# Remainders of projection weights: subtraction on two engines, or an accumulating DMA

## The chip, the cores and the metric

The kernel runs on one core of a Trainium2 chip. The metric is the device time of one execution in microseconds (us), the median of several runs. PE is TensorE (PEld its weight loads), DVE is VectorE, ACT is ScalarE, POOL is GpSimd, SP is SyncE, which here issues DMAs only.

## What is computed

A decoder of two layers for 512 tokens of 1024 columns. Layer 0 is a gated DeltaNet (projections to queries, keys, values and gates, a short convolution, a delta rule over chunks of 64 tokens), layer 1 a sparse attention with three branches over one shared set of keys and values. Each layer is modulated by a condition c. The core of the reference:

```python
for l in range(DEPTH):
    shift, scale, gate = ada_modulation(c, ada_w[l], ada_b[l])
    h = rmsnorm(x, norm_g[l]) * (1.0 + scale) + shift
    if l < N_A_LAYERS:
        out = gated_deltanet_layer(h, a_in_w[l], a_conv_w[l], a_A_log[l], a_dt_bias[l], a_onorm_g[l], a_out_w[l])
    else:
        j = l - N_A_LAYERS
        out = nsa_layer(h, shared, rel_bias, b_in_w[j], b_out_w[j])
    x = x + gate * out
    if l == N_A_LAYERS - 1:
        shared = nsa_shared_kv(x, kv_norm_g, kv_w, cmp_pos_k, cmp_pos_v, cmp_k_w1, cmp_k_w2, cmp_v_w1, cmp_v_w2)
return rmsnorm(x, final_g)
```

In both layers `h @ in_w` and `y @ out_w`, and `s @ kv_w` for the shared keys and values, are the large products: these are the projections that the change is about.

## The kernel before

**A projection's tile.** A projection is made in tiles of 128 columns. The weights of one are 1024 x 128 float32, 512 KB, and lie in SBUF as 128 partitions x 8 blocks x 128. A product of two float32 matrices is made from parts that PE multiplies in one pass: the weights are split into a rounded part `whi` (the type fp32r) and the remainder `wlo` = weights - `whi`, the other operand likewise into a high and a low part. `dense_steps` (L176) then makes 24 products of 128x512 a tile: for each of the 8 blocks whi with the high part (L186), wlo with the high part (L188) and whi with the low part (L190).

**Loading and splitting.** `load_w` (L155) issues the load of the raw weights `wraw` on SP's queue. `split_w` (L160) copies them to `whi` on ACT (L88 is the line of the helper `act`), and subtracts (L85 is the helper `tt`): a half of the blocks on DVE and the other half on POOL; with `on_pool=8`, as for values and queries of layer 0, all on POOL. wraw, whi and wlo have three buffers each; wraw's are shared with pieces `aw` of the modulation's weights.

**Who splits when.** Projections stand in a `chain` of `Ahead` objects (L235). Each is a generator that has two stages before its products: load, then split. When a projection emits its second product, it has the next one of the chain split; at its fourth, the one after the next loaded. `fill(n)` emits n products of the projections waiting in `todo`, among other work: convolutions, the inverse of the chunks' triangular matrices (L750 to L784), the scan, and in layer 1 the attention.

**What sets the order.** PE's order is that in which the code emits (a manual schedule). ACT's is, too, up to L782. The other engines' order is a scheduler's, which simulates the program. Each engine works its own list off in order; a DMA that POOL issues stands in POOL's list.

**The stages.** Up to some 60 us keys are projected; 62 to 105 us values; 105 to 215 us values, gates and queries beside the inverse (from 148 us on DVE does sums of products `arY`, `arX` of the inverse); then the scan; 335 to 407 us x1, the layer's output, of whose tiles the first three are split by a direct call of `split_w` and the other five pass through the chain; 407 to 465 us the shared keys and values; 465 to 790 us attention with 8 tiles of queries and 24 of gates; then the output projection x2.

**Who does not change.** The keys (split apart or by `dense`, with `ahead=False`), the branch gates (`gate_steps`), the first three tiles of x1 and the halves of x2's last tiles call the old way of splitting before and after.

Of the kernel before, what the change touches and what calls it, by code (L numbers as in the profile page):

```python
# [16 lines left out]
T = 512  # L17
# [40 lines left out]
def tile_hybrid_trunk(ctx: ExitStack, tc: tile.TileContext, A, out, dbg=None):  # L58
# [28 lines left out]
    def act(o, i, fn=AF.Copy, **kw):  # L87
        nc.scalar.activation(o, i, fn, **kw)  # L88
# [30 lines left out]
    class Shared:  # L119
        """Small tables of one phase, cut from a tile whose place the other phase takes over."""  # L120
# [39 lines left out]
    def split_w(raw, on_pool=4, parts=None, split=False):  # L160
        hi, lo = parts or (wp.tile([P, KT, P], F32R, name=n, bufs=3) for n in ("whi", "wlo"))
        q = 2 if split else KT
        act(hi[:, :q], raw[:, :q])
        if split:
            nc.vector.tensor_copy(hi[:, q:], raw[:, q:])
        h = KT - on_pool
        if split:
            tt(nc.vector, lo[:, :2], raw[:, :2], hi[:, :2].bitcast(F32), ALU.subtract)
            tt(nc.vector, lo[:, 2:h], raw[:, 2:h], hi[:, 2:h].bitcast(F32), ALU.subtract)
        elif h:  # L170
            tt(nc.vector, lo[:, :h], raw[:, :h], hi[:, :h].bitcast(F32), ALU.subtract)
        if h < KT:
            tt(nc.gpsimd, lo[:, h:], raw[:, h:], hi[:, h:].bitcast(F32), ALU.subtract)
        return hi, lo

    def dense_steps(src, xh, xl, name, on_pool=4, raw=None, parts=None, tag="d", done=None, ahead=True):  # L176
        """W^T x by single-pass products of the parts, one at a time."""
        raw = raw if raw is not None else load_w(src)
        if ahead:
            yield None  # L180
        wh, wl = split_w(raw, on_pool, parts)
        if ahead:
            yield None
        ps = (pd if tag == "d" else pm).tile([P, T], F32, name=name, tag=tag)
        for k in range(KT):
            nc.tensor.matmul(ps, wh[:, k], xh[:, k], start=(k == 0), stop=False)  # L186
            yield ps
            nc.tensor.matmul(ps, wl[:, k], xh[:, k], start=False, stop=False)  # L188
            yield ps
            nc.tensor.matmul(ps, wh[:, k], xl[:, k], start=False, stop=(k == KT - 1))  # L190
            if k == KT - 1 and done:
                done(ps)
            yield ps

    def gate_steps(src, xh, xl, name, done):
        """The branch gates' few columns, the parts of their weights side by side."""
        raw = load_w(src)
        yield None
        w = wp.tile([P, KT, P], F32R, name="whi", bufs=3)
        act(w[:, :, 0:64], raw[:, :, 0:64])  # L200
        tt(nc.vector, w[:, :, 64:128], raw[:, :, 0:64], w[:, :, 0:64].bitcast(F32), ALU.subtract)
        yield None
        ps = pd.tile([P, T], F32, name=name, tag="d")
        for k in range(KT):
            for x in (xh, xl):
                nc.tensor.matmul(ps, w[:, k], x[:, k], start=(k == 0 and x is xh), stop=(k == KT - 1 and x is xl))
                if k == KT - 1 and x is xl:
                    done(ps)
                yield ps
# [8 lines left out]
    def after(n, f):  # L218
        """Leaves f for when n more products of the waiting projections are out."""
        later.append((clock[0] + n, f))  # L220
# [14 lines left out]
    class Ahead:  # L235
        """A projection whose weights are split while the one before it runs."""
# [5 lines left out]
        def go(self, stage):  # L242
            """Up to loaded (1) or split (2) weights."""
            while self.stage < stage:
                next(self.steps)
                self.stage += 1
# [4 lines left out]
        def __next__(self):  # L251
            self.go(2)
            self.n += 1
            if self.n == 2 and self.i + 1 < len(chain):
                chain[self.i + 1].go(2)
            if self.n == 4 and self.i + 2 < len(chain):
                chain[self.i + 2].go(1)
            return next(self.steps)

    def fill(n):  # L260
        """Emits the next n products of the waiting projections."""
        while n > 0 and todo:
            if next(todo[0], None) is None:
                todo.pop(0)
            else:
                n -= 1
                tick()

    def residual(wsrc, h_, l_, gate, xin, xout, name, after, tags="dddddddd"):
        """xout = xin + gate * (W^T y) by column tiles; the sums of squares of all of them but the last, and the last's."""  # L270
        sums = []

        def done(j, ps):
            stt(xout(j), ps, gate[:, j:j + 1], xin(j), ALU.mult, ALU.add)
            sq = tmp(f"{name}sq{j}")
            act(sq, xout(j), AF.Square)
            if 0 < j < KT - 1:
                tt(nc.gpsimd, sums[0], sums[0], sq, ALU.add)
            else:
                sums.append(sq)  # L280
            after(j)

        return [dense_steps(wsrc[j], h_, l_, f"{name}{j}", tag=tags[j], done=partial(done, j)) for j in range(3, KT)], sums, done
# [3 lines left out]
    def rsqrt(dst, src, scale):  # L287
        """dst = (src * scale + eps) ** -0.5 on small tables: a first guess from the exponent, three Newton steps."""
# [23 lines left out]
    def chunk(src, cols, dst):  # L312
        """A block of a weight, all rows by some columns, two row tiles a transfer."""
# [6 lines left out]
    def vec_mat(vec, t, dst, bias, name, between=0):  # L320
        """dst = vec^T W + bias with columns onto partitions: four partial sums side by side, then their transposes."""
# [26 lines left out]
    def ada_piece(space=None):  # L348
        """The modulation's other columns, two row tiles of four column tiles at a time, off the tensor engine."""
# [122 lines left out]
    def shifted(i):  # L472
        """Half of the modulated input."""
# [6 lines left out]
    def again(i):  # L480
        """The keys' weights once more."""
# [56 lines left out]
    def ready(ct):  # L538
        """Waits for a convolved column tile."""
# [87 lines left out]
    def keys(i, part):  # L627
        """Half of the keys, with the shift."""
# [65 lines left out]
    def decay_prep(h, low):  # L694
        """The exponent's size (low) or itself (up) inside the triangle, out of range outside."""
# [55 lines left out]
    with tc.high_priority(offset=400):  # L751
          for b in (2, 4, 8, 16):
              n, st = 16 // b, 66 * b

              def prod(o, i0, i1, right):
                  """o[pair, c, a] = sum over m of i0[pair, a, m] * i1[pair, c, m]; (tile, offset, strides of pair, free, m).
                  The triangle is the right factor, no m under c, or the left one, no m over a."""
# [168 lines left out]
    def scan_norm(G, n0, n1):  # L926
        """The norm of the outputs of some chunks, with the queries' norm."""
# [8 lines left out]
    def scan_turn(n, G):  # L936
        """Heads onto partitions, gated."""
# [46 lines left out]
    with tc.high_priority(offset=300):  # L984
# [30 lines left out]
        def some(j, ks, c, stop):  # L1015
            """A part of a column tile's products."""
# [72 lines left out]
    def key_rows(t, dst):  # L1089
        """Both halves of the partitions get hi, in one copy, and lo, in the other."""  # L1090
# [87 lines left out]
    class Head:  # L1178
# [18 lines left out]
        def softmax(self, qb):  # L1197
            """Scores of a block of queries, with their bias, through the three softmaxes and the branch gates."""
# [39 lines left out]
        def turn(self, qb):  # L1238
            """Keys on partitions, four blocks a bank."""
# [64 lines left out]
    def to_rows(j, n0, n1):  # L1304
        """The last norm's gain, and tokens onto partitions."""
# [33 lines left out]
    def x2_steps(j, parts=None):  # L1339
        """A column tile of the output projection."""  # L1340
# [7 lines left out]
    def early():  # L1348
        """The output projection's first tiles over the pairs that are done."""
# [9 lines left out]
    def x2_halves():  # L1359
        """The last column tiles, half of the tokens after the other."""  # L1360
# [58 lines left out]
    with ordered:  # L1419
# [204 lines left out]
```

## Time and profile before

| | us |
|---|---|
| median of 3 runs (lowest to highest) | 833.56 (833.0 to 839.4) |
| span of the profiled execution | 834.3 |
| PE busy | 759.7 (91%) |
| DVE busy | 598.0 (72%) |
| ACT busy | 404.0 (48%) |
| POOL busy | 370.6 (44%) |
| chain that ended last: PE 65%, DVE 22%, DMA 5% | |

For the profiled execution the span is the only time on record. Busy times are of one execution; an engine that is idle costs nothing unless another waits for it, so the stages and the waits are read beside them. A row's L number is a line of the kernel before; in a row of a timeline the start counts from the span's beginning. A half remainder of 128x512 is a row `wlo<-wraw,whi 128x512`, a whole one `128x1024`.

### The profile page before, as it was taken

Reading aid. Unit: us, or ns where it says so; the run is one execution under the profiler, and the core shown is the slowest. Engines: PE = TensorE matmul, PEld = TensorE weight load, DVE = VectorE, ACT = ScalarE, POOL = GpSimd, SP = SyncE. Lnnn points to the kernel's source line nnn. Section 1 sums busy time; section 2 is a strip of 40 time slices with the busy share of each in tenths; the row PEclk is TensorE's granted clock in tenths of the full one; section 3 lists DMA queues with packets and bytes.
Section 4 is the critical chain, followed back from the end, with each engine's and each line's share of the span. In section 5 each row is a group of like instructions: output and inputs, shape, how many; then the busy total and the mean of one; then the engine's idle time right before and its main releaser. Section 6 shows DMA issues by size and latency. Waiting matters only on the chain.

```text
span 834.3 us, 13577 instructions
## 1 busy us (share of the span) xinstructions
PE 759.7 (91%) x4773; PEld 618.5 (74%) x4773; DVE 598.0 (72%) x1473; ACT 404.0 (48%) x921; POOL 370.6 (44%) x344
## 2 busy tenths in 40 slices
PE   4998779878899997999986999999999999999996
PEld 2675458657788886797774788888888888887876
DVE  2699596897246658879888487777776867768574
ACT  2543646553415553354434285547564745457222
POOL 2365134586733233315389243444444444446150
PEclk9999979899958999999998999999999999999999
DMA  8976133437632143147813432232322232323112
GB/s 305 386 218 213 50 104 79 147 132 199 160 116 76 51 166 113 53 138 223 334 51 112 131 98 90 89 90 71 95 89 63 92 99 80 103 73 115 51 38 101
DMA packets 52852, 104.20 MB, mean 125 GB/s; under 512 B 15930, under 2 KB 24474, under 8 KB 52784
## 3 DMA queue, kind: packets, MB, share of 16 engines
q1 hardware_dynamic: 43392, 97.19, 36.0%
q10 hardware_dynamic: 8720, 4.06, 1.8%
q0 software_dynamic: 672, 2.09, 0.9%
q8 instruction: 37, 0.61, 0.3%
q14 instruction: 31, 0.25, 0.1%
HBM read 97.49 MB, written 7.14 MB: 125 GB/s over the span
## 4 chain that ended last, share of the span: by engine, by line
PE 65%; DVE 22%; DMA 5%; issue 3%; ACT 2%; ACTq 1%; POOL 1%; SPq 0%; DVEq 0%
PE z L186 5%; PE z L190 5%; PE z L188 5%; PE o L1261 4%; PE pt L1245 4%; PE pc L186 3%; PE pc L188 3%; DVE wlo L85 2%; PE pc L190 2%; DVE arY L85 2%; DVE arK L82 2%; PE q L186 2%; PE q L188 2%; PE q L190 2%; DMA wraw<-in_wS 1%
## 5 line engine op out<-in xcount | busy, mean ns | idle before, releaser
L85 POOL TENSOR_TENSOR wlo<-wraw,whi 128x512 fp32r<-128x512 f32 (+2 forms) x84 | 140.3, 1672 | 180.3 <-ACT whi L88 136.9
L88 ACT ACTIVATE arX<-arX,nm 128x256 f32<-128x256 f32 (+3 forms) x128 | 71.2, 556 | 103.2 <-DVE nm L1202 102.5
L79 POOL TENSOR_SCALAR arX<-arX,f 128x256 f32<-128x256 f32 (+3 forms) x128 | 68.8, 550 | 97.8 <-DVE f L85 60.7
L88 ACT ACTIVATE whi<-wraw 128x1024 fp32r<-128x1024 f32 (+2 forms) x85 | 88.2, 1039 | 38.2 <-DMA wraw<-in_wA 11.5
L85 DVE TENSOR_TENSOR wlo<-wraw,whi 128x512 fp32r<-128x512 f32 (+2 forms) x69 | 72.6, 1055 | 11.3 <-ACT whi L88 11.1
L190 PE MATMUL z<-h1l,whi 128*128 128x512 f32 x192 | 76.8, 400 | 0.0
L186 PE MATMUL z<-h1h,whi 128*128 128x512 f32 x192 | 76.6, 399 | 0.0
L188 PE MATMUL z<-h1h,wlo 128*128 128x512 f32 x192 | 75.9, 395 | 0.0
L186 PE MATMUL pc<-xh,whi 128*128 128x512 f32 x128 | 57.3, 448 | 16.4 <-DVE vT L82 8.1
L190 PE MATMUL pc<-xl,whi 128*128 128x512 f32 x128 | 55.2, 431 | 1.1 <-DVE xl L85 1.1
L188 PE MATMUL pc<-xh,wlo 128*128 128x512 f32 x128 | 55.8, 436 | 0.1
L186 PEld LDWEIGHTS pc<-xh,whi 128*128 128x128 f32 x128 | 26.6, 208 | 27.3 <-issue 22.4
L1245 PE MATMUL pt<-ident,arX 128*128 128x128 f32 x320 | 45.3, 272 | 0.0
L1245 PEld LDWEIGHTS pt<-ident,arX 128*128 128x128 f32 x320 | 38.7, 140 | 8.3
L188 PEld LDWEIGHTS z<-h1h,wlo 128*128 128x128 f32 x192 | 36.2, 188 | 6.1
L186 PEld LDWEIGHTS z<-h1h,whi 128*128 128x128 f32 x192 | 36.2, 188 | 5.6
L190 PEld LDWEIGHTS z<-h1l,whi 128*128 128x128 f32 x192 | 36.1, 188 | 5.5
L85 POOL TENSOR_TENSOR ap<-ap,aw 128x512 f32<-128x512 f32 x21 | 31.2, 1485 | 9.9 <-ACT ap L88 7.7
L1202 DVE CUSTOM_DVE_ANT_0 arX<-sw,arY 128x256 f32<-128x256 f32 (+2 forms) x48 | 26.7, 557 | 11.0 <-POOL arX L79 6.6
L1261 PE MATMUL o<-pta,vb 128*64 128x128 f32 x336 | 32.1, 275 | 0.0
L1231 DVE TENSOR_SCALAR f<-sm 128x3 f32<-128x3 f32 x64 | 14.6, 228 | 24.3 <-ACT arX L88 24.1
L190 PEld LDWEIGHTS pc<-xl,whi 128*128 128x128 f32 x128 | 26.6, 208 | 6.7 <-DVE xl L85 1.5
(433 smaller groups left out, 2205.4 us busy)
## 6 DMA issues: line engine op xcount, KB each, us to landing
wraw<-in_wB SPq DMA_DIRECT2D x33, 512.0 KB, 3.3
wraw<-in_wA SPq DMA_DIRECT2D x28, 512.0 KB, 4.6
aw<-in_ada_w SPq DMA_DIRECT2D x20, 512.0 KB, 3.9
arY<-in_ada_w SPq DMA_DIRECT2D x12, 512.0 KB, 4.7
arN<-gcd SPq DMA_DIRECT2D x16, 256.0 KB, 3.8
wraw<-in_wO SPq DMA_DIRECT2D x8, 512.0 KB, 3.4
arY<-rbw SPq DMA_DIRECT2D x64, 64.0 KB, 2.0
wraw<-in_wP SPq DMA_DIRECT2D x8, 512.0 KB, 3.3
```

The costliest lines, as they stand in the source:

```text
L79: eng.tensor_scalar(out=o, in0=i, scalar1=s1, scalar2=s2, op0=op0, op1=op1)
L82: nc.vector.scalar_tensor_tensor(out=o, in0=i, scalar=s, in1=j, op0=op0, op1=op1)
L85: eng.tensor_tensor(out=o, in0=a, in1=b, op=op)
L88: nc.scalar.activation(o, i, fn, **kw)
L186: nc.tensor.matmul(ps, wh[:, k], xh[:, k], start=(k == 0), stop=False)
L188: nc.tensor.matmul(ps, wl[:, k], xh[:, k], start=False, stop=False)
L190: nc.tensor.matmul(ps, wh[:, k], xl[:, k], start=False, stop=(k == KT - 1))
L1202: nc.vector.tensor_tensor_reduce(out=o, in0=ps, in1=bias, op0=ALU.add, op1=ALU.min, scale=1.0, scalar=init, accum_out=acc)
L1231: nc.vector.tensor_scalar_max(f[:, qb], sm[:, qb], 1e-30)
L1245: nc.tensor.transpose(self.ps[:, i], x[:, kb * P:(kb + 1) * P], ident)
L1261: nc.tensor.matmul(po[64 * e:64 * e + 64, qb * P:(qb + 1) * P], vv, pts[2 * pr + e, br, kb, qb], start=(kb == 0), stop=(kb == qb), tile_po ...
```

## The change

`split_w` gets the address of the weights in memory. Where it has it, ACT makes `whi` as before and then a second copy, -whi, into `wlo`; then POOL issues a DMA that reads the weights from memory once more and adds them to `wlo`. The subtractions on DVE and POOL are gone there. `dense_steps` passes the address if the projection is in the chain. And `Ahead` splits the next projection at the first product, the one after it at the second, and loads the third at the fourth. The rest of the diff takes comments out and moves lines by up to 7.

```diff
-    def split_w(raw, on_pool=4, parts=None, split=False):
+    def split_w(raw, on_pool=4, parts=None, split=False, src=None):
         hi, lo = parts or (wp.tile([P, KT, P], F32R, name=n, bufs=3) for n in ("whi", "wlo"))
+        if src is not None:
+            act(hi, raw)
+            act(lo, hi.bitcast(F32), scale=-1.0)
+            nc.gpsimd.dma_start(lo, src, accum_op=ALU.add)
+            return hi, lo
         q = 2 if split else KT
...
-        wh, wl = split_w(raw, on_pool, parts)
+        wh, wl = split_w(raw, on_pool, parts, src=src if ahead else None)
...
             self.go(2)
             self.n += 1
-            if self.n == 2 and self.i + 1 < len(chain):
+            if self.n == 1 and self.i + 1 < len(chain):
                 chain[self.i + 1].go(2)
-            if self.n == 4 and self.i + 2 < len(chain):
-                chain[self.i + 2].go(1)
+            if self.n == 2 and self.i + 2 < len(chain):
+                chain[self.i + 2].go(2)
+            if self.n == 4 and self.i + 3 < len(chain):
+                chain[self.i + 3].go(1)
             return next(self.steps)
```

POOL's list during the inverse, before (`ap` sums pieces of the modulation, `arY` is cleared for what follows the inverse):

```order
L85 TENSOR_TENSOR ap_1159<-ap_1159,arY_634 128x512 x2
L85 TENSOR_TENSOR wlo<-wraw,whi 128x1024
L798 MEMSET arY_634 128x2560
L85 TENSOR_TENSOR ap_1384<-ap_1384,aw_1382 128x512
L85 TENSOR_TENSOR wlo<-wraw,whi 128x512
L85 TENSOR_TENSOR wlo<-wraw,whi 128x1024
L85 TENSOR_TENSOR ap_1384<-ap_1384,aw_1448 128x512 x2
L85 TENSOR_TENSOR wlo<-wraw,whi 128x512
L85 TENSOR_TENSOR ap_1384<-ap_1384,aw_1487 128x512 x2
L85 TENSOR_TENSOR wlo<-wraw,whi 128x1024
```
and after the change:

```order
L85 TENSOR_TENSOR ap_1173<-ap_1173,arY_634 128x512 x2
L805 MEMSET arY_634 128x2560
L165 DMA wlo<-in_wA 128x1024
L85 TENSOR_TENSOR ap_1400<-ap_1400,aw_1398 128x512
L165 DMA wlo<-in_wA 128x1024
L85 TENSOR_TENSOR ap_1400<-ap_1400,aw_1464 128x512 x2
L165 DMA wlo<-in_wA 128x1024
L85 TENSOR_TENSOR ap_1400<-ap_1400,aw_1504 128x512 x2
L806 MEMSET arY_634 128x1536
L165 DMA wlo<-in_wA 128x1024
```
Each remainder of 128x1024 or 128x512 on POOL has become a DMA issue, and so have remainders of which DVE made the other half; the sums of `ap` and the clearing stand between them as before.

ACT's list at x1's first tile that passes through the chain, before (`yh` is the high part of the scan's output, `x1sq` and `sh` follow from the tile of x1 before, `x1d` stores that tile):

```order
L88 ACTIVATE yh<-arX 128x4x128 x2
L88 ACTIVATE whi<-wraw 128x1024
L88 ACTIVATE x1sq_2987<-arK 128x512
L88 ACTIVATE sh<-arK,colp 128x512
L979 DMA x1d<-arK 128x512
L88 ACTIVATE whi<-wraw 128x1024
L88 ACTIVATE ap_2990<-arY_634,csil 128x512
L88 ACTIVATE x1sq_3009<-arK 128x512
```
and after the change:

```order
L88 ACTIVATE yh<-arX 128x4x128 x2
L88 ACTIVATE whi<-wraw 128x1024
L88 ACTIVATE x1sq_3003<-arK 128x512
L88 ACTIVATE sh<-arK,colp 128x512
L986 DMA x1d<-arK 128x512
L88 ACTIVATE wlo<-whi 128x1024
L88 ACTIVATE whi<-wraw 128x1024
L88 ACTIVATE ap_3006<-arY_634,csil 128x512
L88 ACTIVATE x1sq_3025<-arK 128x512
```
The copy to wlo stands behind the two activations and the store that follow the copy to whi, ahead of the next tile's copy to whi.

## Rows read from the trace of the kernel before

**Rows 1.** The page's head and its busy times: TensorE.

```profile
span 834.3 us, 13577 instructions
...
PE 759.7 (91%) x4773; PEld 618.5 (74%) x4773; DVE 598.0 (72%) x1473; ACT 404.0 (48%) x921; POOL 370.6 (44%) x344
```

**Rows 2.** Stages: stretch, length, busy PE, PEld, DVE, ACT, POOL, clock, DMA share, GB/s.

```profile
62.00:88.00 26.00, 20.37 (x101) 13.33 (x103) 25.93 (x33) 9.43 (x15) 11.54 (x7) 0.98 0.56 178
...
101.00:112.00 11.00, 2.92 (x13) 1.04 (x12) 8.98 (x15) 6.79 (x12) 6.89 (x6) 0.63 0.72 235
...
148.00:200.00 52.00, 42.47 (x174) 33.66 (x173) 50.31 (x74) 25.99 (x50) 38.18 (x23) 0.90 0.43 140
...
372.00:407.00 35.00, 31.40 (x148) 25.08 (x146) 32.18 (x39) 14.73 (x21) 18.48 (x12) 1.00 0.74 241
...
465.00:790.00 325.00, 322.65 (x2126) 270.81 (x2125) 237.19 (x849) 183.45 (x523) 140.89 (x179) 1.00 0.28 88
```

**Rows 3.** PE's waits, 105 to 215 us: total, times, longest, in us.

```profile
PE pc L186 <- DVE vT L82: 8.1, 1, 8.1
```

**Rows 4.** Groups by form: busy us, mean ns of one, idle before and releaser.

```profile
L85 DVE TENSOR_TENSOR wlo<-wraw,whi 128x512 fp32r<-128x512 f32 x61 | 64.6, 1058 | 6.2 <-ACT whi L88 6.0
...
L85 POOL TENSOR_TENSOR wlo<-wraw,whi 128x1024 fp32r<-128x1024 f32 x16 | 40.1, 2507 | 41.5 <-ACT whi L88 41.4
...
L88 ACT ACTIVATE whi<-wraw 128x1024 fp32r<-128x1024 f32 x83 | 87.2, 1051 | 31.4 <-DMA wraw<-in_wA 11.5 <-DMA arY<-rbw 6.2 <-PE x L190 5.5
```

**Rows 5.** DVE in order of time: start, us, line, operation, tiles, count.

```profile
63.46 4.10 DVE L79 TENSOR_SCALAR arA<-arA,gs,mod 128x512 f32<-128x512 f32 x4
...
76.37 1.91 DVE L79 TENSOR_SCALAR arA<-arA,gs,mod 128x512 f32<-128x512 f32 x4
...
103.74 4.97 DVE L82 SCALAR_TENSOR_TENSOR arN<-arN,pha 128x128 f32<-128x128 f32 x4 [2.02 <-DMA arN<-gcd]
...
110.08 4.29 DVE L82 SCALAR_TENSOR_TENSOR arN<-arN,pha 128x128 f32<-128x128 f32 x8
...
172.95 1.22 DVE L85 TENSOR_TENSOR arY<-arX 128x1024 f32<-128x1024 f32 x1
...
192.77 3.05 DVE L85 TENSOR_TENSOR arY<-arX,arY 128x1024 f32<-128x1024 f32 x1
```

**Rows 6.** POOL in order of time, same columns: two DMA issues and a remainder.

```profile
2.02 0.55 POOL L396 DMA_DIRECT2D rbt<-in_rb  x1
...
162.43 1.07 POOL L967 DMA_DIRECT2D oneh<-in_oneh  x2
...
190.56 3.41 POOL L85 TENSOR_TENSOR wlo<-wraw,whi 128x1024 fp32r<-128x1024 f32 x1
```

**Rows 7.** DMA: a queue's packets, MB, share; issues, KB each, median us to landing.

```profile
q1 hardware_dynamic: 43392, 97.19, 36.0%
...
wraw<-in_wB SPq DMA_DIRECT2D x33, 512.0 KB, 3.3
...
wraw<-in_wS SPq DMA_DIRECT2D x4, 512.0 KB, 12.1
```

**Rows 8.** Stages, wlo's instructions alone: PE, PEld, DVE, POOL, clock, DMA share, GB/s.

```profile
148.00:200.00 52.00, 21.57 (x52) 10.62 (x51) 4.56 (x3) 14.65 (x7) 0.90 0.43 140
...
465.00:790.00 325.00, 108.26 (x274) 51.60 (x274) 33.78 (x33) 48.38 (x33) 1.00 0.28 88
```

**Rows 9.** x1's first tile, ACT and PE in order of time.

```profile
371.49 1.06 ACT L88 ACTIVATE whi<-wraw 128x1024 fp32r<-128x1024 f32 x1 [2.33 <-PE x L1023]
...
374.56 0.40 PE L186 MATMUL x<-yh,whi 128*128 128x512 f32 x1
...
374.79 0.40 PE L188 MATMUL x<-yh,wlo 128*128 128x512 f32 x1
```

**Rows 10.** The chain of waits, 372 to 465 us: start, us, what.

```profile
385.28 6.17 DMA arY<-in_ada_w
...
431.71 1.75 DVE wlo L85
```


## What I expect, before any run of the changed kernel

> **What bounds the kernel now.** I read first the busy times, then the stages, then the waits of TensorE (PE) and the chain of waits inside the stages where PE is not full. PE is busy for 759.7 us of a span of 834.3 us [rows 1], so all that any change off PE can win is the 74.6 us in which PE has nothing to do. The stages say where these lie [rows 2]. From 465 to 790 us (attention) PE is busy for 322.65 of 325 us at full clock: nothing is to be had there. From 62 to 88 us PE is busy for 20.37 of 26 us and DVE for 25.93; from 148 to 200 us PE for 42.47 of 52 and DVE for 50.31. In both the reader is to see a DVE that never rests while PE does: there DVE sets the time. From 101 to 112 us PE does 2.92 us of work: it stands for 8.1 us behind one DVE instruction [rows 3]. From 372 to 407 us both are nearly full (31.40 and 32.18 of 35 us) and the DMA engines are at 0.74 of their time.
>
> What the change takes off DVE and POOL is plain work: 61 halves of 1.058 us on DVE, 16 whole remainders of 2.507 us on POOL [rows 4], and POOL's halves. And where POOL's remainder lies beside a DVE instruction, the DVE instruction is long: four tensor_scalar took 4.10 us at 63.46 us and 1.91 us at 76.37 us; a 128x1024 sum of two tiles took 3.05 us beside POOL's remainder of 190.56 us, against 1.22 us for the like product of 172.95 us; four instructions on arN took 4.97 us with such a remainder and three sums on POOL, against 4.29 us for eight just after [rows 5, 6]. So a POOL remainder costs DVE most of its own length when DVE happens to be there.
>
> **The change part by part.** 72 tiles change: 24 of values, gates and queries, 5 of x1, 6 of keys and values, 32 of the second layer's queries and gates, 5 of x2. In each, a half of 1.06 us on DVE and one on POOL (or 2.5 us of POOL alone) go; one more ACT copy of 128x1024 comes, 1.051 us by the like copy to whi [rows 4]; one DMA issue on POOL comes, 0.55 us by the plain issue at 2.02 us [rows 6]; and 512 KB more are read from memory. None of it is work for PE, so the price is the time from the raw weights to the remainder, and the ways it gets into.
>
> The accumulating transfer itself is nowhere in this trace. Below stands the plain load of the same bytes, 3.3 us from issue to landing; above, the same bytes in the crowd of the start, 12.1 us [rows 7]. It is nearer the first, since these tiles mostly move at a DMA share well under 0.75. But it must also read what it adds to. Queue q1 moved 97.19 MB in 36.0% of the span [rows 7], so 512 KB cost 1.62 us of all 16 engines; I add this once for the second reading and take **D = 4.9 us**. From raw weights to remainder that makes 1.05 + 1.05 + 0.55 + 4.9 = 7.6 us, where before it was at most 1.05 and 2.5. A page of the Trainium skill, "DMA: Bandwidth & Descriptors" (section "Anatomy of one DMA — SWDGE (gpsimd) path"), gives a transfer issued by GpSimd 2.0 us and its bytes at 436 GB/s; for 512 KB that is 3.2 us, an estimate for plain bytes, and no run here shows an accumulating one. By it the only term to move would be the stall at x1's first tile below, by 1.7 us.
>
> The stages, with their terms:
>
> *62 to 88 us: -4.* Two of POOL's remainders lie beside DVE here, and each made a DVE piece about 2.2 us longer (4.10 - 1.91; the other at 71.69 us reads alike) [rows 5]. DVE is the stage's bound, so I count both. Above: nothing, if PE's own work is next; PE idles 5.6 us there, so 4 fit.
>
> *101 to 112 us: -2.5.* PE waits for DVE's instruction on vT, which stands behind the arN piece [rows 3, 5]. At the later instructions' rate four take 2.1 us and not 4.97; the two sums of arN on POOL remain near, so 2.5 of the 2.8.
>
> *148 to 200 us: -6.* Own work: three halves, 4.56 us of DVE [rows 8]. Beside POOL: two pairs of this stretch, 1.8 us (3.05 - 1.22) and about as much in the other, at 169.41 us [rows 5]. That is 8.1 us of a DVE that is the bound; PE's idle time there, 9.5 us, would take it. Against it stand more than seven new ACT copies of 1.05 us in ACT's fixed order between the instructions that DVE waits for; they take back between 0 and 7 us. ACT has half of the stretch free, so I give them 2. POOL's remaining additions still lie beside DVE as before.
>
> *372 to 407 us: +2.* x1's first tile has no lead: its whi copy ends at 372.55 us and its first product with wlo runs at 374.79 us [rows 9]. By the order on ACT the copy to wlo comes only behind two more activations and one DMA issue, so behind about 374 us; with issue and D the remainder lands at about 375 + 0.55 + 4.9 = 380.5 us, 5.7 us late. PE idles 3.6 us of this stretch anyway, and the stage's DVE work goes on meanwhile and is relieved of 4 us; I let 2 us remain. Ends: -2 and +5.7. The one row that shows POOL issuing beside a busy DVE has two transfers in 1.07 us at 162.43 us, no longer than the 0.55 us of one at the start [rows 6]. A rule of the Trainium skill speaks against the change here: "SBUF — State Buffer" (section "🔬 SBUF: two separate sides") says that while VectorE runs an instruction of the kind that takes its second pair of ports, GpSimd can't write the descriptors of its DMAs, which then wait. By the rule this term would be about +4, with one piece of DVE's (1.91 us) in the way; the row, where DVE ran other kinds of instruction, doesn't decide it.
>
> *407 to 465 us: -3.* DVE's half of 1.75 us at 431.71 us lies on the chain of waits [rows 10], a second lies there with 0.55 us, and POOL's two halves beside them go too.
>
> *Crowding: +2.* In 372 to 407 us two loads of modulation columns lie on the chain, 6.17 us the longest [rows 10], with the DMA engines at 0.74. One accumulating transfer ahead of each makes it longer by half to all of 1.62 us.
>
> *465 to 790 us: 0.* 274 products with wlo are 34.25 tiles [rows 8], one in 9.5 us; two ahead are 19 us of lead against 7.6. What hides it all is PE's own work. If D grew, this cover would go (below). ACT gets 34 copies, 36 us, and DVE and POOL lose 34 and 48; none of the three is the bound.
>
> Sum: -4 - 2.5 - 6 + 2 - 3 + 2 + 0 = -11.5 us, so 834.3 - 11.5 = 822.8. The profiled execution's span is 834.3 us, 0.7 above the median of 833.56 (833.0 to 839.4), which hangs together with the profile alone; I take it off: **822 us**.
>
> **The rivals.** *Absorbed (no change).* DVE's relief in the stages is taken by POOL's other additions, which now lie where its remainders lay, and by ACT's copies in the fixed order; for it: ACT and POOL feed DVE in each of these stages; against it: PE waits on DVE by name [rows 3]. With half of the 15.5 us lost and the 4 us of costs kept, -3.7: 830 us, and 826 to 834 with the bounds of x1's stall.
>
> *Slower: the transfer is the cycle's length.* Three buffers of wlo go round: a tile's buffer is free when its last product ends, then come two copies, issue and D, and then its own turn. A tile can't come oftener than every (2.65 + D + time of a tile's products) / 3. The products of attention's tiles take 9.5 us, so it holds from (2.65 + D + 9.5) / 3 = 9.5, D = 16 us; where tiles stand close, 24 products of 0.23 us (those of 374.56 and 374.79 us [rows 9]) make 5.5 us, and it holds from D = 8.4 us. At D = 12.1 [rows 7] only the close tiles, some 20 of them, would wait, by (2.65 + 12.1 + 5.5) / 3 - 5.5 = 1.2 us each: 24 us less what DVE's relief wins, 822 + 24 = 846. At D = 20 attention's 34 tiles add 1.2 us each, 41 more: 887. It decides from D of about 11 us. For it: this trace shows no accumulating transfer, so nothing excludes such a D. Against it: the mean DMA share of 0.36 on q1 leaves room for twice the traffic.
>
> *All of it converts.* Without x1's stall and with DVE's whole relief, 4 + 2.8 + 8.1 + 4 + 4 in 372 to 407 us, -23: 811 us; PE's idle time allows it, nothing suggests that all waits are DVE's.
>
> **How the numbers follow.** My forecast (-11.5, with ends -7 and -17 from the terms' bounds) 0.45; absorbed 0.27; slower by the cycle or by a longer stall at x1 0.2; all converts 0.08. The likeliest gives 822, with a range of its own from 816 to 827. The range to hold 8 in 10 leaves out half of the last and half of the slower: 809 to 843. One per cent of the median, 8.3 us, is about what a measurement can tell: faster is under 825.2, slower over 841.9. My forecast is faster in four fifths of its cases, and all of the last are: 0.36 + 0.08 and a little of the absorbed, 0.47. Slower takes 0.17 of the slower rival and little else, 0.18; the rest is the same, 0.35.
>
> **What would show it.** Right: the DVE pieces of 63.46, 103.74 and 192.77 us shorter by 2 to 3 us each, DVE's busy time down by some 60 to 90 us; accumulating transfers that land in 4 to 6 us; attention's 325 us within 2; PE waiting for a DMA at x1's first product with wlo for 3 to 6 us. Wrong: landings over 10 us, products with wlo that wait for a DMA again and again, or ACT's copies named as the releaser of DVE in 148 to 200 us.

## The result, and the profile after

The changed kernel takes 840.52 us (median of 16 runs), before it 836.31 us over as many: a ratio of 1.0064, with a 95% interval of 1.0037 to 1.009. So it is slower by 0.6%, where 1.4% faster was forecast. The ratio leaves out the executions that count as slow, here one of 958.37 us at a granted clock of 0.743. (Over more runs the median of before has come out at 836.3 and not 833.6; experiments below are given by their ratio to before.)

The page after, its head, the busy times and the two DMA queues (packets, MB, share of 16 engines' span). From here on a row's L number is a line of the kernel that it comes from: the products L186, L188 and L190 of before are L191, L193 and L195 after.

```profile
span 838.2 us, 13563 instructions
...
PE 756.2 (90%) x4773; PEld 617.5 (74%) x4773; DVE 525.6 (63%) x1417; ACT 470.7 (56%) x993; POOL 304.2 (36%) x344
...
q1 hardware_dynamic: 43392, 97.19, 35.3%
...
q0 software_dynamic: 11040, 39.84, 26.9%
```

DVE lost 72 us of work and POOL 66, ACT gained 67, as the diff says; the span grew by 4. TensorE's matmuls come in the same order in both, so each can be set beside itself. This is the start of the same product in both traces, worked out from the timelines of PE:

```
product                     before     after   difference
value tile 2, first wlo       95.4      92.4      -3.0
value tile 3, first whi      109.5     104.0      -5.5
value tile 7, first wlo      145.2     139.5      -5.7
third query tile, whi        203.1     192.1     -11.1
gate tile, last products     214.9     210.9      -4.0
query tile, whi              254.8     243.0     -11.9
queries by keys              261.1     254.8      -6.3
gate tile                    326.8     319.7      -7.1
x1, first chained tile       374.8     376.6      +1.8
kv, first tile, first whi    407.3     407.6      +0.3
kv, second tile, a whi       415.6     422.2      +6.7
kv, fourth tile, sixth       426.3     444.8     +18.6
transposes of vbT            448.9     455.1      +6.3
attention, start             485.9     490.1      +4.3
attention, end               730.9     734.2      +3.4
```

Up to 203 us 11 us are won. From 203 to 215 us 7 are lost, around 250 us the same stretch runs at another clock (last section), which by 327 us has given 3 of them back, at x1 9 are lost and at the keys and values another 4 to 5 in the end. Attention moves by 1.

The DVE pieces that stood beside POOL's remainders, as they are now (start, us; answers to the first, third and last of [rows 5]):

```profile
64.11 1.91 DVE L79 TENSOR_SCALAR arA<-arA,gs,mod 128x512 f32<-128x512 f32 x4
...
101.13 2.09 DVE L82 SCALAR_TENSOR_TENSOR arN<-arN,pha 128x128 f32<-128x128 f32 x4 [2.33 <-DMA arN<-gcd]
...
178.87 2.00 DVE L85 TENSOR_TENSOR arY<-arX,arY 128x1024 f32<-128x1024 f32 x1
```

1.91 us for 4.10, 2.09 for 4.97, 2.00 for 3.05: the first two are shorter by what was costed, the last by 1.05 us of 1.8. What PE waits for now (us in total, times, longest; the vT row answers to [rows 3]):

```profile
PE kv L193 <- DMA wlo<-in_wKV: 14.4, 2, 10.8
...
PE x L193 <- DMA wlo<-in_wO: 9.7, 2, 8.7
...
PE pc L191 <- DVE vT L82: 5.5, 1, 5.5
...
PE pz L193 <- DMA wlo<-in_wA: 3.6, 2, 3.3
```

27.7 us of waiting for an accumulating DMA, at six products. The issues (KB each, median us from the issue's start to landing; the plain ones answer to [rows 7]):

```profile
wraw<-in_wB SPq DMA_DIRECT2D x33, 512.0 KB, 3.9
...
wlo<-in_wB POOLq DMA_DIRECT2D x32, 512.0 KB, 5.6
...
wlo<-in_wA POOLq DMA_DIRECT2D x24, 512.0 KB, 8.0
...
wlo<-in_wKV POOLq DMA_DIRECT2D x6, 512.0 KB, 7.7
...
wlo<-in_wO POOLq DMA_DIRECT2D x5, 512.0 KB, 9.0
```

and the stages in which it is late or crowded, with attention (columns as in [rows 2], stretches counted in the kernel after):

```profile
200.00:219.00 19.00, 14.78 (x163) 12.11 (x163) 3.62 (x5) 12.69 (x18) 8.90 (x8) 0.82 0.99 237
...
372.00:407.00 35.00, 29.44 (x121) 23.83 (x122) 18.86 (x28) 15.81 (x20) 10.90 (x10) 0.87 1.02 297
...
465.00:790.00 325.00, 323.16 (x2138) 270.81 (x2137) 198.05 (x810) 216.41 (x559) 121.47 (x180) 1.00 0.64 149
```

From 372 to 407 us the DMA share went from 0.74 to 1.02, and DVE's work from 32.18 to 18.86 us without PE being any faster.

x1's first chained tile, on ACT, POOL and PE in order of time (answers to [rows 9]):

```profile
364.45 1.06 ACT L88 ACTIVATE whi<-wraw 128x1024 fp32r<-128x1024 f32 x1 [2.33 <-PE x L1030]
...
366.55 1.04 ACT L88 ACTIVATE wlo<-whi 128x1024 fp32r<-128x1024 f32 x1
...
367.89 0.91 POOL L165 DMA_DIRECT2D wlo<-in_wO  x1 [7.90 <-PE x L1030]
...
376.60 0.80 PE L193 MATMUL x<-yh,wlo 128*128 128x512 f32 x1 [8.70 <-DMA wlo<-in_wO]
...
377.20 0.63 PE L195 MATMUL x<-yl,whi 128*128 128x512 f32 x1
```

The copy to wlo ends at 367.6, the transfer is issued 0.3 us later and is waited for until 376.60: 8.7 us for issue and transfer. Then products take 0.63 us where they took 0.40 [rows 9]: PE had stood since 367.9 us, and from 371 to 381 us the granted clock is 0.50, the lower of its two levels (1.2 GHz for 2.4).

And the fourth tile of the keys and values (ACT, then POOL, then the chain of waits):

```profile
425.17 0.69 ACT L88 ACTIVATE rs<-x1ss,epst 128x512 f32<-128x512 f32 x1 [11.73 <-PE x1ss L1447]
...
425.87 1.06 ACT L88 ACTIVATE whi<-wraw 128x1024 fp32r<-128x1024 f32 x1
...
428.77 1.05 ACT L88 ACTIVATE whi<-wraw 128x1024 fp32r<-128x1024 f32 x1
...
429.73 1.99 ACT L88 ACTIVATE wlo<-whi 128x1024 fp32r<-128x1024 f32 x2
...
428.95 5.45 POOL L85 TENSOR_TENSOR arK<-arK,rs 128x512 f32<-128x512 f32 x4 [16.17 <-ACT rs L88]
...
434.37 3.38 POOL L85 TENSOR_TENSOR arY<-tk,pos 128x496 f32<-128x496 f32 x2
...
437.69 0.86 POOL L165 DMA_DIRECT2D wlo<-in_wKV  x1
...
437.69 5.24 DMA wlo<-in_wKV
...
373.98 9.70 DMA arY<-in_ada_w
```

PE had begun this tile at 431.8 us and stood from then to 442.97. ACT's list holds the copy to whi (425.87 us) behind `rs`, which waits for PE's sums of squares; another tile's copy stands between it and the copy to wlo, the first of the two from 429.73 us; POOL's list holds the issue behind two pieces of other work, so that it goes out at 437.69 us, 7 us after the copy, and lands at 442.9. The last row, from the stage before, is a load of modulation columns on the chain, 9.70 us where the longest was 6.17 [rows 10].

### The profile page after: what moved, and what is told of

Read it like the earlier page. It is cut to its first block, busy times and chain, and to the rows that moved or that the text cites. A ratio compares the mean times of both kernels' runs of the same rounds, so it can differ in the third digit from the quotient of the medians.

```text
span 838.2 us, 13563 instructions
## 1 busy us (share of the span) xinstructions
PE 756.2 (90%) x4773; PEld 617.5 (74%) x4773; DVE 525.6 (63%) x1417; ACT 470.7 (56%) x993; POOL 304.2 (36%) x344
## 3 DMA queue, kind: packets, MB, share of 16 engines
q0 software_dynamic: 11040, 39.84, 26.9%
## 4 chain that ended last, share of the span: by engine, by line
PE 62%; DVE 15%; DMA 10%; issue 5%; ACT 3%; POOL 2%; SPq 1%; ACTq 0%; DVEq 0%; POOLq 0%
PE z L191 5%; PE z L193 5%; PE z L195 5%; PE o L1268 4%; PE pt L1252 4%; DMA arY<-in_ada_w 3%; DVE arK L82 2%; PE q L193 2%; PE q L191 2%; PE q L195 2%; DMA wlo<-in_wA 2%; PE pc L193 2%; DVE arN L82 1%; PE pc L195 1%; PE pc L191 1%
## 5 line engine op out<-in xcount | busy, mean ns | idle before, releaser
L88 ACT ACTIVATE wlo<-whi 128x1024 fp32r<-128x1024 f32 x70 | 73.6, 1054 | 8.5 <-issue 7.6
L195 PE MATMUL z<-h1l,whi 128*128 128x512 f32 x192 | 76.9, 400 | 0.0
L191 PE MATMUL z<-h1h,whi 128*128 128x512 f32 x192 | 76.6, 399 | 0.0
L193 PE MATMUL z<-h1h,wlo 128*128 128x512 f32 x192 | 75.9, 395 | 0.0
L191 PE MATMUL pc<-xh,whi 128*128 128x512 f32 x128 | 54.8, 428 | 12.7 <-DVE vT L82 5.5
L193 PE MATMUL pc<-xh,wlo 128*128 128x512 f32 x128 | 54.1, 423 | 1.0 <-DMA wlo<-in_wA 1.0
L165 POOL DMA_DIRECT2D wlo<-in_wA x24 | 21.7, 905 | 88.5 <-ACT wlo L88 36.2
L195 PE MATMUL pc<-xl,whi 128*128 128x512 f32 x128 | 53.2, 416 | 0.0
L165 POOL DMA_DIRECT2D wlo<-in_wB x32 | 27.8, 870 | 47.6 <-ACT wlo L88 33.5
L191 PEld LDWEIGHTS pc<-xh,whi 128*128 128x128 f32 x128 | 25.4, 199 | 22.6 <-issue 12.1
L193 PEld LDWEIGHTS z<-h1h,wlo 128*128 128x128 f32 x192 | 36.1, 188 | 6.1
L191 PEld LDWEIGHTS z<-h1h,whi 128*128 128x128 f32 x192 | 36.2, 188 | 5.5
L195 PEld LDWEIGHTS z<-h1l,whi 128*128 128x128 f32 x192 | 36.1, 188 | 5.5
L1238 DVE TENSOR_SCALAR f<-sm 128x3 f32<-128x3 f32 x64 | 12.7, 198 | 42.0 <-ACT arX L88 42.0
L85 POOL TENSOR_TENSOR ap<-ap,aw 128x512 f32<-128x512 f32 x21 | 28.7, 1366 | 26.5 <-ACT aw L88 17.7
L85 POOL TENSOR_TENSOR wlo<-wraw,whi 128x256 fp32r<-128x256 f32 (+1 forms) x14 | 17.0, 1224 | 48.3 <-ACT whi L88 37.9
L193 PE MATMUL kv<-sh,wlo 128*128 128x512 f32 x48 | 20.8, 434 | 14.4 <-DMA wlo<-in_wKV 14.4
```

The source lines that it names most:

```text
L85: eng.tensor_tensor(out=o, in0=a, in1=b, op=op)
L165: nc.gpsimd.dma_start(lo, src, accum_op=ALU.add)
L1238: nc.vector.tensor_scalar_max(f[:, qb], sm[:, qb], 1e-30)
```

## Experiments

**The two late stages.** Theory *late* says that the gain made early is lost where remainders come after their turn, *traffic* that the second readings slow everything, *lead* that splitting two ahead costs by itself.

e1: x1, keys and values the old way, the rest as changed.

```diff
-        wh, wl = split_w(raw, on_pool, parts, src=src if ahead else None)
+        wh, wl = split_w(raw, on_pool, parts, src=src if ahead and name.startswith(('pc', 'pz', 'q', 'z', 'x2')) else None)
```

> The changed kernel, but x1's five tiles and the six of keys and values are subtracted by DVE and POOL as before; the two-ahead chain stays. Theory late (the gain made up to 205 us is lost where a remainder lands after its turn, at x1's first tile 8.7 us and at two kv tiles 14.4 us, with TensorE slow for some us after each): about 8 us under before, 824 to 830. Theory traffic (72 second readings slow all transfers, the stalls only show it): 61 readings remain, so at most a sixth of the loss goes, 834 to 840. Theory lead (splitting two ahead costs by itself): as the changed kernel, 836 to 842.

Measured 827.41 us, 0.9886 (0.9812 to 0.996). Theory late holds: undoing 11 of 72 tiles turns 0.6% slower into 1.1% faster.

e8: the reverse, only `('x1', 'kv')` accumulate.

> Accumulating transfers for the 11 tiles of x1 and of keys and values alone, old subtractions elsewhere, two-ahead chain. Theory late: the stalls without the gain, 8 to 16 us over before (842 to 852), with x1's first wlo product and kv's waiting for a DMA as in the changed kernel. Theory traffic: 11 of 72 readings, within 3 us of before, and stalls under half as long.

858.85 us, 1.0252 (1.0172 to 1.0332), above the range. PE's waits for accumulating transfers in it:

```profile
PE kv L193 <- DMA wlo<-in_wKV: 15.6, 2, 11.0
...
PE x L193 <- DMA wlo<-in_wO: 8.3, 1, 8.3
```

They are as long as in the changed kernel, with 61 second readings fewer: those of other stages are not what makes them long. The time beyond my range is the lead's, as the next run says:

e2: the chain of the change, the old subtractions (`split_w(raw, on_pool, parts)`).

> The old subtractions everywhere, and only the two-ahead chain of the change. Theory late and theory traffic: within 3 us of before, since no row of before has a product waiting for a remainder for more than 2.7 us. Theory lead: 3 to 8 us over before.

846.82 us, 1.0118 (1.004 to 1.0196): a miss for my theory. Two ahead is a loss of its own where DVE and POOL subtract. One place is about 200 us, where PE waits for POOL's sums of the modulation; attention, below, is another:

```profile
PE as L382 <- POOL ap L85: 8.8, 2, 7.9
```

e8 lies 1.3% above e2, which is x1, keys and values.

e5: only layer 0's `('pc', 'pz')` accumulate.

> Accumulating transfers for the 24 tiles of values, gates and queries of layer 0 alone, old subtractions elsewhere, two-ahead chain. Theory late: as e1 within 2 us (824 to 830), since attention's 32 tiles have cover and neither win nor lose. If attention's tiles win by themselves, e1 is lower than this one; if their traffic costs, higher. Theory traffic: two thirds of the traffic are gone, so clearly under e1.

836.09 us, 1.0002 (0.9961 to 1.0043), a miss too: 1.2% over e1, with 37 transfers fewer (attention's 32 and x2's 5). In attention PE waits for the softmax's maximum:

```profile
PE sw L1200 <- DVE nm L1209: 5.1, 5, 2.6
```

where before has 0.6 us of this wait. So attention with the lead of two is as fast as before only if the halves leave DVE and POOL.

e13: as e5, but the chain is two ahead only in layer 0 (its first 24 projections), one ahead, as before, later:

```diff
+            two = lambda j: j < len(chain) and j < 24
-            if self.n == 1 and self.i + 1 < len(chain):
+            if self.n == 1 and two(self.i + 1):
...
-            if self.n == 2 and self.i + 2 < len(chain):
+            if self.n == 2 and self.i + 1 < len(chain):
+                chain[self.i + 1].go(2)
+            if self.n == 2 and two(self.i + 2):
...
```

> As e5 (accumulating transfers in layer 0 alone), but the chain splits two ahead there only and one ahead, as before, in every later projection. Theory lead-harms-subtractions (old subtractions two ahead cost attention 7 to 8 us, since DVE and POOL then do them ahead of the softmax): attention as before, 6 to 9 us under e5, so as e1: 824 to 830. If e5's loss in attention has another cause: as e5, 833 to 838.

829.32 us, 0.9912 (0.9875 to 0.9949), as expected: in attention it is the lead, not the transfers. By the starts of the same products attention loses 6.6 us in e5 (from 485.9 to 731 us of before) and nothing in e13. The traces say in part how the lead makes DVE late. In both, DVE stands 1.5 to 1.9 us at a time for a load of a piece `aw` of the modulation, whose buffers are wraw's. In e13 this lies mostly 21 to 25 us ahead of the products that wait for a maximum in e5, and PE doesn't wait; once it lies 8 us ahead, and PE waits 0.6 us. In e5 most of these loads go out 14 to 17 us later in the program, so it lies 8 us ahead four times (PE waits 0.6 to 0.7 us each) and once 2 us (2.6 us). That makes 4.5 of the 6.6 us; no run has moved these loads alone.

**One late stage at a time.** e15 (x1 alone the old way) and e16 (keys and values alone), by the same line as e1.

> The changed kernel with x1's five tiles alone subtracted as before. By the trace of the changed kernel x1's first tile cost 8.9 us of wait and 1.8 us of slow clock, of which 3 were made good by 407 us: so 7 to 9 us under the changed kernel if x1's wait is a loss of its own; within 2 us of it if the time won at x1 is only waited for again at the keys and values.

> The changed kernel with the six tiles of keys and values alone subtracted as before. Between 407 and 450 us the changed kernel lost 5 us net against before (3.6 + 10.9 of waits and 4 of slow clock, against 8.2 that before spends waiting for vbT and some more): so 4 to 6 us under the changed kernel if the two stages add up to e1's 13 us, and within 2 us of it if DVE's chain behind x1ss sets that stage's end anyway.

e15: 836.7 us, 1.0 (0.9963 to 1.0037); e16: 834.32 us, 0.9981 (0.995 to 1.0011). Against 1.0064 these are 0.6% or 5 us for x1, somewhat under what I expected, and 0.8% or 7 us for the keys and values, a little over. They add up to e1's 1.8% within the intervals, which are wide: 0.4% on e15, 0.3% on e16. The traces don't add up like that. From x1's first chained tile to the end the changed kernel loses 10.9 us on before, e16 6.5, e15 still 9.5 and e1 nothing. In e15 the kv tiles wait longer than in the changed kernel:

```profile
PE kv L193 <- DMA wlo<-in_wKV: 17.2, 2, 11.0
```

There the time won at x1 is in large part waited for again at the keys and values, as e15's second case has it. That both places together cost what e1 gives back is shown; how much is x1's alone is not.

**Is it POOL's list or the transfer?** e10 gives two pieces of POOL's other work to DVE:

```diff
-                tt(nc.gpsimd, sums[0], sums[0], sq, ALU.add)
+                tt(nc.vector, sums[0], sums[0], sq, ALU.add)
...
-        tt(nc.vector if k % 2 else nc.gpsimd, x1[:, k], x1[:, k], rs1, ALU.mult)
+        tt(nc.vector, x1[:, k], x1[:, k], rs1, ALU.mult)
```

> The changed kernel, with two pieces of POOL's other work given to DVE: the sums of x1's squares and the scaling of the modulated input (four products of 128x512, 5.45 us, that stood in POOL's list ahead of the keys' and values' accumulating transfers). Theory list (the 10.8 us wait of kv was for POOL's list: its copy to wlo was done at 431.7 us, the transfer was issued at 437.69 us): the issue follows its copy within 1.5 us, the wait shrinks to 4 to 6 us, x1's first wait (issued 0.3 us after its copy, landing 8.7 us later) stays, and the time is 4 to 6 us under the changed kernel: 832 to 838. Theory transfer (it is the transfers alone that are slow): waits and time as in the changed kernel, within 3 us.

838.5 us, 0.9988 (0.9938 to 1.0037). The median of all ten runs is 2 us under the changed kernel's, the ratio, which leaves out the four longest, 0.8% or 6 us: the time doesn't decide between the theories. PE's wait, and POOL at the place, do:

```profile
PE kv L193 <- DMA wlo<-in_wKV: 12.4, 2, 7.8
...
427.94 3.08 POOL L85 TENSOR_TENSOR arY<-tk,pos 128x496 f32<-128x496 f32 x2 [17.38 <-DVE tk L85]
...
430.97 1.76 POOL L165 DMA_DIRECT2D wlo<-in_wKV  x2
```

The longest wait is 7.8 us and not 10.8. The copy to wlo now ends at 428.9 us and the issue follows after 2 us and not 7, as theory list has it; but the transfer then takes 7.2 us (PE's product starts at 438.1) where it took 5.24, so 3 us are left of the 5. The rest of the wait is ACT's list and the transfer, so POOL's list made about 3 of the 10.8 us.

**What makes the transfer slow.** e6 takes `accum_op` away; e7 reads the raw weights in SBUF:

```diff
-            nc.gpsimd.dma_start(lo, src, accum_op=ALU.add)
+            nc.gpsimd.dma_start(lo, raw, accum_op=ALU.add)
```

> The changed kernel with plain transfers in place of accumulating ones: wlo is overwritten with the whole weights, so the subtraction is left out; the traffic from memory is the same. If the accumulation costs a second pass, a plain transfer takes about half of the DMA engines' time (1.6 us of all 16 against 3.1) and lands in 3.3 to 5 us where the accumulating one took 5.6 to 9.0; if only POOL's way of issuing is slow, landings stay at 5.6 to 9.0 us.

```profile
q0 software_dynamic: 11040, 39.84, 15.7%
...
wlo<-in_wB POOLq DMA_DIRECT2D x32, 512.0 KB, 4.4
...
wlo<-in_wA POOLq DMA_DIRECT2D x24, 512.0 KB, 6.1
...
wlo<-in_wKV POOLq DMA_DIRECT2D x6, 512.0 KB, 4.7
...
wlo<-in_wO POOLq DMA_DIRECT2D x5, 512.0 KB, 7.0
```

The queue's share is 15.7% of 822.1 us against 26.9% of 838.2. Less the 7.5 us that it has for other things (0.9% in before), a plain transfer costs 1.7 us of all 16 engines, an accumulating one 3.0. It lands 1.2 to 3 us earlier. The one time taken is 824.33 us. But PE waits at both late stages all the same:

```profile
PE kv L193 <- DMA wlo<-in_wKV: 9.9, 2, 9.0
...
PE x L193 <- DMA wlo<-in_wO: 8.1, 1, 8.1
```

At x1 that is 8.1 us for 8.7, at the keys and values 9.9 for 14.4. So the accumulation makes the transfers long, but by this one execution most of the two stalls is there with plain transfers as well (in x1's stage, 356 to 391 us in e6, the DMA share is 0.87).

> The changed kernel, whose accumulating transfer reads the raw weights from SBUF and not once more from memory. If memory's second reading makes the transfers slow, they land in 3 to 4.5 us, the stalls at x1 and kv shrink by 3 to 5 us each, and the time is 6 to 12 us under the changed kernel. If the accumulation itself and POOL's list are slow, landings and stalls stay within 1 us, and the time within 4 us of the changed kernel's.

```profile
q0 software_dynamic: 11040, 39.84, 24.5%
...
wlo<-wraw POOLq DMA_DIRECT2D x70, 512.0 KB, 5.5
...
PE as L382 <- POOL ap L85: 13.3, 1, 13.3
...
SPq L366 <- DMA wlo<-wraw: 92.3, 13, 11.5
```

857.36 us, 1.0212 (1.0106 to 1.0317): neither theory. 24.5% of 856.9 us is 2.8 us of all engines a transfer, so in the engines' time the accumulation is what costs, and the second reading from memory next to nothing. At x1's first tile alone PE waits 5.9 us and not 8.7; whether that is the source or another crowd, no run separates. The time is lost elsewhere: wraw's buffers are now held until the transfer is through, the modulation's pieces share them, SP's loads of these pieces (L366) wait for the transfers, and PE stands 13.3 us for one.

**Is the lead needed?** e9: e1 with the chain of before. e3: the changed kernel with the chain of before.

> As e1 (accumulating transfers but for x1, keys and values), with the chain of before: split one ahead, load two ahead. From raw weights to remainder the changed kernel took 1.05 + 1.05 + 0.9 + 5.6 (attention) to 8.0 us (layer 0), so 8.6 to 11. Theory lead-needed: in layer 0 a tile's lead is 5.5 us where tiles stand close, so products wait for a DMA in several of the 24 tiles, some 3 us each, and little is left of e1's gain: 830 to 850; attention, one tile in 9.5 us, waits little. Theory lead-harms (it is the lead that costs, as in e2, and the transfers need none): under e1, 815 to 825.

> The changed kernel with the chain of before. Theory lead-needed: on top of e9 each of x1's five and the six kv tiles waits some 4 to 6 us for its remainder: 20 to 40 us over e9. Theory lead-harms: not over the changed kernel.

e9: 854.09 us, 1.0225 (1.0143 to 1.0308), lead needed, and more of it than I thought:

```profile
PE pc L193 <- DMA wlo<-in_wA: 15.6, 5, 7.2
...
PE pz L193 <- DMA wlo<-in_wA: 9.9, 2, 6.0
```

25.5 us of waits in layer 0. e3: 863.84 us, 1.0338 (1.027 to 1.0406), 10 us over e9 where I expected 20 to 40: x1's and kv's waits are those of the changed kernel (9.2 and 13.9 us), so at these two places the lead of two gives nothing.

**A version that beats both.** After 200 us DVE has time in layer 0 (it works for 5.96 of 19 us in before's stage) and, in the changed kernel, the DMA engines have none (0.99). e11: as e1, but only layer 0's first 14 tiles accumulate there. e14: these 14 alone, two ahead for them alone (e13 with 14 for 24).

> As e1, but layer 0's last ten tiles (from the fourth gate on, so from about 205 us, where DVE has little to do) are subtracted as before too. Theory late: the loss of 4 to 7 us between 188 and 217 us in e1, with the DMA engines at 0.91 of their time, goes in part: 2 to 5 us under e1. If that loss is the clock or ACT's list alone: within 2 us of e1.

> As e13, with accumulating transfers and the lead of two in layer 0's first 14 tiles alone; all later tiles as before the change. By the two theories of e11 and e13: 2 to 5 us under e13 if the crowding past 200 us costs, else within 2 us; 820 to 828 in all.

e11: 823.91 us, 0.9858 (0.9788 to 0.9928); e14: 822.83 us, 0.9846 (0.9771 to 0.992). e14's median is 6.5 us under e13's and e11's 3.5 under e1's, with intervals that overlap. The traces are clearer: between the products that start at 203.1 and 216.4 us in before, e1 and e13 lose 5.5 and 6.9 us, e11 and e14 1.3 and 1.5. So the loss past 200 us goes with the ten transfers there. 14 transfers give all of the gain that 72 were to give.

```profile
span 818.5 us, 13580 instructions
...
200.00:280.00 80.00, 79.71 (x751) 67.67 (x750) 43.06 (x66) 32.91 (x60) 34.85 (x24) 0.87 0.34 101
...
200.00:280.00 80.00, 72.04 (x692) 60.93 (x693) 38.34 (x55) 36.88 (x57) 25.55 (x22) 0.85 0.58 142
```

In the same 80 us (the head and the first stretch are e14's, the last is the changed kernel's; columns as in [rows 2]) the DMA share is 0.34 against 0.58, PE busy for 79.71 against 72.04 us.

## Right and wrong, by the prediction's steps

*The early gain* was right, and nearly in size. 62 to 88 us: -4 forecast; a key's product at 62.8 us stood at 63.4 after, and the table has -3.0 at 95 us, so -3.6. 101 to 112 us: -2.5 and -2.5; PE's wait for vT is 5.5 us for 8.1 [rows 3]. 148 to 200 us: -6 and -5.4. Together -12.5 and -11.5. A part was over-read: the sum of 192.77 us was set beside one of another form (1.22 us), so 1.8 us was counted for it, and it fell by 1.05. What ACT's new copies cost by themselves (2 us forecast) no run isolates.

*203 to 215 us* had no term, and lost 7 us: 3.6 us of waits of gate tiles for their remainders and a clock of 0.82 (200 to 219 us) where before has 1.00, with the DMA engines at 0.99. I had counted traffic as a cost in one stage only. e11 and e14 keep most of this gain.

*x1's first tile* failed, in two ways. The copy and the issue went as read off ACT's order, but issue and D took 8.7 us and not 0.55 + 4.9, so that the wait was 8.7 us where 5.7 was expected; and I let 3.7 of it vanish in PE's idle time, which did not happen: net 9 us at the place, 7.3 by 407 us, against 2 + 2 for stall and crowding (by e15's median 5 of it are x1's alone, by its trace less). Crowding was too small as well: the longest load of modulation columns took 9.70 us for 6.17, where at most 1.62 more was counted.

*Keys and values* failed by sign: -3 forecast, +4 in the table, 7 by e16. I took the two halves off DVE's path and did not ask by which way the remainder would come instead. The chain's lead of two says how far ahead a split is emitted, not when it runs: the copy to whi stands in ACT's list behind `rs` in both kernels. Before, the halves were there 3 us after that copy's start; now two more copies, POOL's list and the transfer follow, 17 us from 425.87 to 442.97.

*D* is the term under both. 4.9 us was the plain load plus one reading; measured are 5.6 in attention, 8.0 in layer 0, 9.0 and 7.7 at x1 and the keys, each with its issue of 0.9 us. The engines' time was sized well (3.2 by my 1.62 twice, 3.0 measured); what I left out is the other transfers: e6's plain ones took 4.4 us in attention, with a DMA share of 0.46, and 7.0 at x1, with 0.87. The rule of the Trainium skill in "DMA: Bandwidth & Descriptors" (section "🔬 Anatomy of one DMA — SWDGE (gpsimd) path"), by which 512 KB would take 3.2 us (an estimate), is under the plain transfer's 4.4 us in e6 as well; the measurement decides. The rule of the Trainium skill in "SBUF — State Buffer" (section "🔬 SBUF: two separate sides"), that GpSimd can't write descriptors while DVE runs an instruction that takes its second pair of ports, is neither borne out nor excluded by a run here.

*Attention* was right at 0, but half by luck: the lead alone costs 7 us there (e5 against e13), the halves' leaving gives it back.

*The rival* "slower by the cycle or by a longer stall at x1" is what came, by its second half, and with it the keys and values, which no rival named; its first half, D over 11 us with three buffers, did not. That 840.5 us still lies in the range of 809 to 843 is due to the rivals' ends and not to the terms of the forecast.

## To carry to other kernels

A longer way to a result needs its lead checked at each place where the stream of tiles starts anew or where a copy stands in an engine's list behind something late: a look-ahead in the program's order is no lead there. Use the slow path where there is lead and where the engine that it relieves is the bound, and the old one elsewhere; here 14 of 72 tiles bring the whole gain. And price a transfer by how full the DMA engines are in its stage, not by the median of quiet stages.

## What I had not expected of the hardware

An accumulating transfer of 512 KB took 3.0 us of all 16 DMA engines where a plain one by the same queue took 1.7, and reading its source from SBUF changed that little (2.8). Between 200 and 280 us the granted clock came out at 0.81 before, 0.85 after and 0.87 in e14, though PE's products are the same and come in the same order: the table's difference goes from -4.0 to -11.9 and back to -6.3 us there. Such a stretch alone moves some us between kernels, so a term of that size is better read from the start of the same product on both sides of its stage than from the whole time.
